# Whole branches for one and for two token tiles in the expert steps of a hybrid trunk block, with other orders for the first and last step

## The chip, the cores and the metric

The kernel runs on one core of a Trainium2 chip. The metric is the device time of one execution in microseconds (us). PE is the matrix engine, ACT, DVE and POOL are the scalar, vector and GpSimd engines, SP issues the weight loads; each runs its own queue of instructions in order and waits for the others by semaphores.

## The reference

One layer of a block on 2048 tokens of width 1024: a mixer (Mamba-2 heads beside mLSTM heads), then a mixture of experts, then a norm. Only the experts are touched here:

```python
p_group = softmax(x32 @ wg + bg); pg, g_sel = top_k(p_group, 1)
e_in = (x32 @ we + be).reshape(t, 4, 8)[:, g_sel]        # 4 groups of 8 experts
top_v, top_i = top_k(e_in, 2); gates = softmax(top_v) * pg
ids = (g_sel * 8 + top_i).reshape(-1); order = argsort(ids); xs = xf[order // 2]
hg = ragged_dot(xs, w_gate, sizes); hu = ragged_dot(xs, w_up, sizes)     # 1024 -> 512
ys = ragged_dot(silu(hg) * hu, w_down, sizes)                            # 512 -> 1024
y = segment_sum(ys * gates, tok);  out = rmsnorm(x + y, norm_f_w)
```

## The kernel before

**Tiles.** Each of the 32 experts gets the tokens that chose it in tiles of 128. All have a first tile; how many have a second is known only on the chip. `ns[i]` counts an expert's tokens in blocks of 64: over 2 there is a second tile, and at 3 only half of it is filled. A test of `ns[i]` is a branch that PE, ACT, DVE and POOL each take on their own. The trace shows which tests were taken: no second tile for experts 0 to 7, 10, 11, 13, 14, 16, 24, 27 and 29, a full one for 21 and 22, a half one for the rest.

**Weights.** Each expert has 12 pieces of 512 KB (8 of gate and up, 4 of down). SP loads a piece into one of RAW = 6 buffers (`mraw`), ACT casts it (`hi`, L652), DVE subtracts the cast (`lo`, L653): float32 products are made of three passes (hi times hi, hi times lo, lo times hi; `passes`, L763). For a half second tile two products suffice (`both`, L775). WK = 14 pairs of hi and lo are held.

**Steps.** `manual_schedule` keeps the written order on every engine. Step i runs the letters of ORDER (HEAD for i = 0, LAST for i = 31); each letter issues a piece of work on all engines concerned, and a dot feeds one weight piece (cast and subtract). In a step, A and C are the two halves of the first tile's gate and up products (24 products each), B and D those of the second tile. H turns (transposes on PE, L753, then splits the result into hi on ACT, L237, and lo on DVE, L238) the previous expert's activations h, K those of the second tile. X turns the gathered tokens `xg0` of the next expert, Y those of its second tile. a and b are the activations of the first and second tile (b of a half tile ends on POOL, L791). d and e are the two halves of the previous expert's down product, g those of its second tile; results are copied to `pv`. P adds `pv` to the token rows in memory (`accd`, L837), Q does so for the second tile. F gathers the tokens of expert i + 2 into `xg0` and, behind a test, `xg1` (L740, L880); E reads its count. r, s and m finish the rows of an earlier group of experts, 256 at a time: r gathers them (`f`), s makes their squares on ACT (L827) and the factor r on DVE and POOL (L833, L195, L201 to L204), m scales on DVE (L929) and writes.

**Skipped tests.** B, K, D, b, Y, g, Q and F hold a test each:

```python
            def whole_or_half(k, full, half):
                with tc.If(ns[k] > 2):
                    with tc.If(ns[k] < 4) as c:
                        half()
                    with c.Else():
                        full()
```

Where a test on PE is not taken, PE's sequencer runs a semaphore instruction that brings the count of PE's products up to where the skipped ones would have brought it (L1048 EVENT_SEMAPHORE in the trace).

Of the kernel before, what the change touches and what calls it, by code (L numbers as in the profile page):

```python
# [8 lines left out]
F32 = mybir.dt.float32  # L9
# [27 lines left out]
RAW, WK = 6, 14  # L37
ENGS = (mybir.EngineType.PE, mybir.EngineType.Activation, mybir.EngineType.DVE, mybir.EngineType.Pool)

ORDER = '.A.EB.HKC..r.Xa..D.b.dYePFzsg..Qm'  # L40
HEAD = 'AEBX....C.ar....D.bdYeF'
LAST = 'HKd..e..PgQ..tA..B..C...uayDhkbdKlejfvogwxq'
NQ = 4
FIRST, START = 6, 8
WB = 5
# [7 lines left out]
def hybrid_block_kernel(ctx, tc, x, norm1_w, w_in, ssd_conv_w, ssd_conv_b, ssd_dt_bias, ssd_a_log,  # L53
# [25 lines left out]
    def sc(shape, name):  # L79
        return ps_s.tile(shape, F32, name=name, tag="sc")  # L80
# [552 lines left out]
    def moe(x1, x1s, rs):  # L633
# [105 lines left out]
        def gather(dst, src, at):  # L739
            return G.indirect_dma_start(out=dst, out_offset=None, in_=src,  # L740
                                        in_offset=bass.IndirectOffsetOnAxis(ap=at, axis=0),
                                        bounds_check=S - 1, oob_is_err=False)

        def pair(n, name):
            return [mp.tile([128, n, 128], F32R, name=name + p) for p in "hl"]

        def turn(dst, src):

            hi, lo = dst
            for q in range(hi.shape[1] // 4):  # L750
                p = sc([128, 4, 128], "mt")
                for k in range(4):
                    PE.transpose(p[:, k, :], src[:, (4 * q + k) * 128:(4 * q + k) * 128 + 128], ident)  # L753
                split(hi[:, 4 * q:4 * q + 4, :], lo[:, 4 * q:4 * q + 4, :], p)

        def entry(at):
            en = mp.tile([128, 8], I32, name="en", bufs=10)
# [101 lines left out]
        def pull_down():  # L859
            return [p for u in pull(2) for p in u]  # L860
# [10 lines left out]

        def fetch(i):

            d = gather(xgs[0], x1d, eti[:, 0, seq[i]:seq[i] + 1])
            if i:
                fetch1(i)
            return d

        def fetch1(i):
            with tc.If(ns[i] > 2):  # L880
                gather(xgs[1], x1d, ens[i][1][0])

        d = fetch(0)
        for f in lows[:4]:
            f()
        xs[0] = [pair(KD, "x") for t in range(2)]
        turn(xs[0][0], xgs[0])
        for f in lows[4:]:
            f()
        feed(START - FIRST)  # L890
# [9 lines left out]
            with c.Else():  # L900
                turn(xs[0][1], xgs[1])
        fetch(1)
        sq = mp.tile([128, 2], F32, name="sq", bufs=1)
        V.memset(sq, 1.0)
        for t in pvs[1:] + fs:
            G.memset(t, 0.0)
# [47 lines left out]
            group_rows(g, q)  # L954


        gl, NW = NG - 1, 4
        sql, rl = (mp.tile([128, 2 * NQ], F32, name=n, bufs=1) for n in ("sql", "rl"))
        enl = mp.tile([128, 2 * NQ, 8], I32, name="enl", bufs=1)
        fl, gt = [], []  # L960
# [44 lines left out]
        def last_more():  # L1005
# [3 lines left out]
            with tc.If(ng > n):  # L1009
# [4 lines left out]
                for t in range(2):  # L1014
# [2 lines left out]
                    apart(d, outs)  # L1017
                    outs.append(d)

        def expert_out():  # L1020

            def second(f):
                with tc.If(ns[NE - 1] > 2):  # L1023
                    f(1)
# [7 lines left out]
            second(lambda t: square(pvs[t], sq[:, t:t + 1]))  # L1032
            norm(r, sq, False)
            out_rows(0)
            second(out_rows)

        def parts(i):

            j = i - 1
            late, cur = i > 0, i < NE  # L1040
            if i + 1 < NE:
                xs[i + 1] = [pair(KD, "x") for t in range(2)]
            w, wd = [], []
            fin = 0 <= group(i)[0] < NG - 1 and group(i)[1] < NQ
            rows = (lambda t: gt[t]) if j == NE - 1 else lambda t: None
# [8 lines that stand above are left out]
            def upper(t, q):  # L1054
                if t == 0:
                    w[:] = pull_up()
                    up(0, xs[i][0], w, q)
                else:
                    whole_or_half(i, lambda: up(1, xs[i][1], w, q), lambda: up_half(xs[i][1], w, q))

            def act1():
                whole_or_half(i, lambda: act(1, hs[i][1], ens[i][1]), lambda: act_half(hs[i][1], ens[i][1], V if i == NE - 1 else G))

            def turn_h():
                ht[j] = [pair(4, "h") for t in range(2)]
                turn(ht[j][0], hs[j][0])

            def act0():
                hs[i] = [mp.tile([128, T], F32, name="h") for t in range(2)]
# [23 lines left out]
            return dict(  # L1093
                E=(i + 2 < NE, lambda: entries(i + 2)), F=(i + 2 < NE, lambda: fetch(i + 2)),
                A=(cur, lambda: upper(0, 0)), B=(cur, lambda: upper(1, 0)), C=(cur, lambda: upper(0, KD // 2)),
                D=(cur, lambda: upper(1, KD // 2)), b=(cur, act1), a=(cur, act0), X=(i + 1 < NE, turn_x),
                Y=(i + 1 < NE, lambda: whole_or_half(i + 1, lambda: turn(xs[i + 1][1], xgs[1]),
                                                     lambda: turn_half(xs[i + 1][1], xgs[1], KD))),
                H=(late, turn_h), K=(late, lambda: whole_or_half(j, lambda: turn(ht[j][1], hs[j][1]),
                                                               lambda: turn_half(ht[j][1], hs[j][1], 4))),  # L1100
                d=(late, lambda: downer(0)), e=(late, lambda: downer(1)), g=(late, down_second),
                P=(late, lambda: puti(j, 0)), Q=(late, put1), r=(fin, lambda: group_count(i)),
                s=(fin, lambda: group_norm(*group(i))), m=(fin, lambda: group_out(*group(i))), z=(1 < i < 6, lambda: enlist(en, sl, i - 2, 2)), t=(True, last_rows), u=(True, last_rows2),
                y=(True, lambda: last_squares(0, 1)), k=(True, lambda: last_squares(2)),
                l=(True, lambda: last_squares(3, 4, 5)), j=(True, lambda: square(pvs[0], sq[:, 0:1])),
                f=(True, last_norm), v=(True, lambda: last_out((0, 1))), w=(True, lambda: last_out((2, 3))),
                x=(True, lambda: last_out((4, 5))), o=(True, last_more), q=(True, expert_out))

        held = 0
        for i in range(NE):  # L1110
            acts = parts(i)
            if i == NE - 2:
                last_entries()
            if i == NE - 1:
                end = parts(NE)
            for c in ORDER if 0 < i < NE - 1 else LAST if i else HEAD:
                if c == ".":
                    feed(min(1, WK - len(ahead) - held))
                    continue
                if c == "h":  # L1120
                    acts["H"], acts = end["H"], dict(end, D=acts["D"], b=acts["b"])
                    c = "H"
                ok, f = acts[c]
                if ok:
                    f()
                    held += {"A": 4, "C": 4, "d": 2, "e": 2, "B": -4, "D": -4, "g": -4}.get(c, 0)
# [374 lines left out]
```

## Time and profile before

| | |
|---|---|
| median of 3 runs | 2982.71 us (2981.85 to 2984.62) |
| profiled execution | 2980.81 us, span 2979.0 us |
| mean granted clock of PE | 0.982 of full speed |
| PE busy over the span | 94% |
| DVE, ACT, POOL busy | 71%, 50%, 22% |
| experts | from 2079 us to the last product at 2953 us |

A matrix product is pipelined: the trace gives 0.39 us for one of 512 columns, but in a dense row the starts lie 0.23 us apart. A bracket at the end of a timeline row is the time in which the engine had nothing to do ahead of it, with what ended that time; PEq is PE's own sequencer. The first products of the steps that are spoken of start at 2101.70 (step 1), 2392.84 (13), 2464.75 (16), 2546.62 (19), 2577.82 (20), 2791.26 (27) and 2846.42 us (29).

### The profile page before, as it was taken

To read this page: it belongs to the slowest core of one execution; us is meant where nothing else is said; L and a number is where in the kernel's file an instruction comes from. 1 tells how busy PE (TensorE), PEld (TensorE's weight loads), DVE (VectorE), ACT (ScalarE), POOL (GpSimd) and SP (SyncE) were. 2 spreads that over 40 slices of the span, in tenths; PEclk is the share of its full clock that TensorE was granted. 3 is DMA by queue.
4 is the path that set the end of the run, shared out by engine and by line. 5 is a ranking of instruction groups with operands and counts; after the bars stand their busy time and mean duration, and the time that the engine had idled before them with its cause. 6 is when DMAs were issued, how large, how long until landed. Compare 5 with 4: busy or idle time off the path is not lost. (4 is left out here: it accounts for less than half of the span.)

```text
span 2979.0 us, 41255 instructions
## 1 busy us (share of the span) xinstructions
PE 2803.4 (94%) x13444; PEld 2219.6 (75%) x13444; DVE 2130.0 (71%) x4043; ACT 1488.4 (50%) x2330; POOL 669.2 (22%) x723
## 2 busy tenths in 40 slices
PE   7999999999999999999999999998889899999995
PEld 5778877777887777788787778786667677787764
DVE  6796487688658678855867875675777777757774
ACT  5544345454434544543454454443666666655663
POOL 1431010362101035200004510001122422421433
PEclk9999999999999999999999999998999999999998
DMA  4222322422322242232224122134898998978993
GB/s 152 69 67 90 92 77 73 140 81 71 92 78 78 78 155 59 71 99 73 84 72 163 50 92 93 57 101 149 300 317 300 292 310 290 295 228 270 295 305 103
DMA packets 228916, 436.52 MB, mean 147 GB/s; under 512 B 38591, under 2 KB 38667, under 8 KB 228640
## 3 DMA queue, kind: packets, MB, share of 16 engines
q1 hardware_dynamic: 206640, 380.88, 38.8%
q0 software_dynamic: 22000, 52.22, 6.6%
q8 instruction: 142, 2.33, 0.3%
q14 instruction: 134, 1.10, 0.1%
HBM read 400.84 MB, written 54.95 MB: 153 GB/s over the span
## 5 line engine op out<-in xcount | busy, mean ns | idle before, releaser
L653 DVE TENSOR_TENSOR lo<-mraw,hi 128x1024 fp32r<-128x1024 f32 x384 | 454.9, 1231 | 80.9 <-ACT hi L652 68.0
L240 ACT ACTIVATE whi<-raw,pcol 128x512 fp32r<-128x512 f32 x416 | 295.0, 721 | 346.5 <-PE acc L278 147.0
L241 DVE SCALAR_TENSOR_TENSOR wlo<-raw,pcol,whi 128x512 fp32r<-128x512 f32 x416 | 318.7, 781 | 199.3 <-ACT whi L240 198.6
L652 ACT CAST hi<-mraw 128x1024 fp32r<-128x1024 f32 x384 | 383.6, 1052 | 79.6 <-DMA mraw<-in_exp_w_up_dram 37.0
L276 PE MATMUL acc<-hh,whi 128*128 128x512 f32 x896 | 365.3, 408 | 0.8 <-ACT whi L240 0.8
L276 PE MATMUL acc<-hh,wlo 128*128 128x512 f32 x896 | 356.8, 400 | 7.6 <-DVE wlo L241 7.6
L276 PE MATMUL acc<-hl,whi 128*128 128x512 f32 x896 | 359.8, 402 | 0.0
L278 PE MATMUL acc<-whi,hh 128*128 128x512 f32 x768 | 311.0, 405 | 2.0 <-ACT craw L289 2.0
L278 PE MATMUL acc<-whi,hl 128*128 128x512 f32 x768 | 310.2, 404 | 0.0
L278 PE MATMUL acc<-wlo,hh 128*128 128x512 f32 x768 | 308.5, 404 | 0.0
L278 PE MATMUL acc<-whi,mh 128*128 128x512 f32 x512 | 204.4, 399 | 0.0
L278 PE MATMUL acc<-whi,ml 128*128 128x512 f32 x512 | 203.4, 397 | 0.0
L278 PE MATMUL acc<-wlo,mh 128*128 128x512 f32 x512 | 203.2, 398 | 0.0
L276 PEld LDWEIGHTS acc<-hh,wlo 128*128 128x128 f32 x896 | 168.9, 189 | 45.7 <-DVE wlo L241 10.2
L290 POOL COPY hist<-craw 128x3 f32<-128x3 f32 x112 | 40.5, 362 | 717.9 <-ACT craw L289 717.6
L276 PEld LDWEIGHTS acc<-hh,whi 128*128 128x128 f32 x896 | 169.4, 189 | 34.5 <-issue 3.1
L276 PEld LDWEIGHTS acc<-hl,whi 128*128 128x128 f32 x896 | 169.6, 189 | 32.2 <-issue 2.6
L288 POOL COPY craw<-hist 128x3 f32<-128x3 f32 x112 | 70.2, 630 | 477.0 <-DVE ir L427 361.2
L278 PEld LDWEIGHTS acc<-whi,hh 128*128 128x128 f32 x768 | 146.2, 190 | 35.6 <-ACT craw L289 3.8
L278 PEld LDWEIGHTS acc<-wlo,hh 128*128 128x128 f32 x768 | 145.6, 190 | 35.2 <-DVE wlo L241 2.0
L278 PEld LDWEIGHTS acc<-whi,hl 128*128 128x128 f32 x768 | 146.2, 190 | 31.8 <-issue 1.0
L837 POOL DMA_INDIRECT accd<-pv,eti x46 | 85.6, 1860 | 356.4 <-ACT hi L652 140.3
(431 smaller groups left out, 6147.6 us busy)
## 6 DMA issues: line engine op xcount, KB each, us to landing
raw<-in_w_in_dram SPq DMA_DIRECT2D x208, 512.0 KB, 3.6
mraw<-in_exp_w_gate_dram SPq DMA_DIRECT2D x128, 512.0 KB, 6.5
mraw<-in_exp_w_up_dram SPq DMA_DIRECT2D x128, 512.0 KB, 7.1
mraw<-in_exp_w_down_dram SPq DMA_DIRECT2D x128, 512.0 KB, 5.6
raw<-in_w_out_dram SPq DMA_DIRECT2D x64, 512.0 KB, 3.6
xi<-in_x_dram SPq DMA_DIRECT2D x16, 512.0 KB, 5.9
x<-in_x_dram SPq DMA_DIRECT2D x4, 2048.0 KB, 8.7
accd<-x SPq DMA_DIRECT2D x16, 512.0 KB, 5.1
```

The source lines that it names most:

```text
L240: A.activation(hi, src, AF.Copy, scale=w)
L241: V.scalar_tensor_tensor(lo, src, w, hi.bitcast(F32), op0=OP.mult, op1=OP.subtract)
L276: mm = PE.matmul(acc[i], b[:, s], a, start=f, stop=e)
L278: mm = PE.matmul(acc[i], a[:, s], b, start=f, stop=e)
L288: G.tensor_copy(raw[:, 0:3], hist[:, ct, :])
L290: h = G.tensor_copy(hist[:, ct, :], raw[:, T:T + 3])
L652: A.copy(hi, raw)
L653: low = lambda: V.tensor_tensor(lo, raw, hi.bitcast(F32), op=OP.subtract)
L837: return G.indirect_dma_start(out=accd, out_offset=bass.IndirectOffsetOnAxis(ap=en[0], axis=0), in_=pvs[t], in_offset=None, bounds_check=S ...
```

## The change

Per step the tests on PE become two. `uppers` (c) holds the first tile's second half, and in its branch for two tiles the turn of the second tile's tokens and both halves of its products. `downers` (n) holds the previous expert's downs, and in the branch for two tiles the turn of the second h and its downs. Both branches contain the first tile's work, written twice. The second tile's gather leaves F and is issued behind c of its own step's predecessor (G). b stands behind n. HEAD turns the next tokens on PE (T) ahead of C and splits them (S) behind a, with six dots ahead of C; a Silu on two numbers is put ahead of the experts, and two of the early subtractions wait for the first gather. At the end all six tiles of the last group are multiplied by the norm's weight early (two of them on POOL), and squares and stores stand in another order.

```diff
-ORDER = '.A.EB.HKC..r.Xa..D.b.dYePFzsg..Qm'
-HEAD = 'AEBX....C.ar....D.bdYeF'
-LAST = 'HKd..e..PgQ..tA..B..C...uayDhkbdKlejfvogwxq'
+ORDER = '.A.E.H.cG.r.Xa...nbPFzs...Qm'
+HEAD = 'AEB......TCaS.r...D.bGF'
+LAST = 'HKd.Ze.PgQ..tA..B..C....uayDhkbpdKlejfgv+owxq'
...
-            d = gather(xgs[0], x1d, eti[:, 0, seq[i]:seq[i] + 1])
-            if i:
-                fetch1(i)
-            return d
+            return gather(xgs[0], x1d, eti[:, 0, seq[i]:seq[i] + 1])
...
-        for f in lows[:4]:
-            f()
+        for n, f in enumerate(lows[:4]):
+            low = f()
+            if n > 1:
+                after(low, [d])
...
+        V.memset(sq, 1.0)
+        A.activation(sq, sq, AF.Silu)
...
-        gl, NW = NG - 1, 4
+        gl, NW = NG - 1, 2 * NQ - 2
...
-                    V.tensor_tensor(fl[t], fl[t], nf, op=OP.mult)
+                    (V if t < 4 else G).tensor_tensor(fl[t], fl[t], nf, op=OP.mult)
...
+            def branch(k, two, one):
+
+                with tc.If(ns[k] > 2) as c2:
+                    with tc.If(ns[k] < 4) as c:
+                        two(True)
+                    with c.Else():
+                        two(False)
+                with c2.Else():
+                    one()
+
+            def uppers():
+
+                w2 = pull_up()
+
+                def one():
+                    up(0, xs[i][0], w2, KD // 2)
+
+                def two(half):
+                    if half:
+                        turn_half(xs[i][1], xgs[1], KD)
+                    else:
+                        turn(xs[i][1], xgs[1])
+                    one()
+                    for q, ww in ((0, w), (KD // 2, w2)):
+                        if half:
+                            up_half(xs[i][1], ww, q)
+                        else:
+                            up(1, xs[i][1], ww, q)
+                branch(i, two, one)
+
+            def downers():
+
+                wd.extend(pull_down())
+                wd.extend(pull_down())
+
+                def one():
+                    for n in range(2):
+                        down(0, ht[j][0], wd[4 * n:4 * n + 4], n)
...
+                branch(j, two, one)
...
+            ps = []
+
+            def split_x():
+                for q, p in enumerate(ps):
+                    turn_split(xs[i + 1][0], q, p)
...
+                T=(True, lambda: ps.extend(turned(xgs[0], q) for q in range(2))), S=(True, split_x),
...
+                c=(cur, uppers), n=(late, downers), G=(i + 1 < NE, lambda: fetch1(i + 1)),
...
-                l=(True, lambda: last_squares(3, 4, 5)), j=(True, lambda: square(pvs[0], sq[:, 0:1])),
+                p=(True, lambda: last_squares(3)), l=(True, lambda: last_squares(4, 5)),
+                j=(True, lambda: square(pvs[0], sq[:, 0:1])),
```

PE in a step of the middle, before: the end of D's branch (products into `pg_18328` and `pu_18329`, the second tile), all of b's test, and the first down product into `pyd_18330`.

```order
L763 MATMUL pu_18329<-hi,xl 128x512
L763 MATMUL pu_18329<-lo,xh 128x512
L1049 UNCONDITIONAL_BRANCH
L1048 UNCONDITIONAL_BRANCH
L1048 COMPARE_AND_BRANCH
L1049 COMPARE_AND_BRANCH
L1049 UNCONDITIONAL_BRANCH x2
L1048 UNCONDITIONAL_BRANCH
L763 MATMUL pyd_18330<-hi,hh 128x512
```

The same place of the changed kernel: the last products of c's branch for one tile, the test of G, the turn of the next tokens, and the head of n with its branch for a half tile.

```order
L768 MATMUL pu_18327<-hi,xl 128x512
L768 MATMUL pu_18327<-lo,xh 128x512
L1068 UNCONDITIONAL_BRANCH
L882 COMPARE_AND_BRANCH
L882 UNCONDITIONAL_BRANCH x2
L750 MATMUL mt<-ident,xg_18063 128x128 x8
L1068 COMPARE_AND_BRANCH
L1069 COMPARE_AND_BRANCH
L802 MATMUL mt<-ident,h 128x64 x4
L768 MATMUL pyd_18330<-hi,hh 128x512
```

Between the turn of the tokens and the downs one test is left, and its two outcomes both hold the downs.

ACT in a step that finishes rows of a group, before: the squares of `f` (s), then the second tile's copies of `pv` (g). The second tile's activation (b) is issued 16 rows ahead of the first of these.

```order
L923 COMPARE_AND_BRANCH
L827 ACTIVATE o,sq<-f_18324 128x1024
L827 ACTIVATE o,sq<-f_18325 128x1024
L923 UNCONDITIONAL_BRANCH x2
L1048 COMPARE_AND_BRANCH
L1049 COMPARE_AND_BRANCH
L804 COPY pv_18323<-pyd_18330 64x512
L804 COPY pv_18323<-pyd_18331 64x512
```

After: the copies of n's branch end, then b (L791 to L795 for a half tile, L815 for a full one), then the squares.

```order
L826 COPY pv_18322<-pyd_18330 128x512
L1068 UNCONDITIONAL_BRANCH
L1053 COMPARE_AND_BRANCH
L1054 COMPARE_AND_BRANCH
L791 COPY h<-pg_18328 64x512
L792 ACTIVATE u<-pu_18329,etf 64x512
L795 ACTIVATE h<-h,etf 64x512
L1054 UNCONDITIONAL_BRANCH
L815 ACTIVATE h<-pg_18328,etf 128x512
L1054 UNCONDITIONAL_BRANCH
L1053 UNCONDITIONAL_BRANCH
L929 COMPARE_AND_BRANCH
```

Here b and the squares have moved behind all copies of the step's down products.

ACT in the first step, before: the split of the next tokens (`xh`), five casts, the table of the Silu, and the activation a.

```order
L1049 UNCONDITIONAL_BRANCH x2
L1048 UNCONDITIONAL_BRANCH
L237 CAST xh<-mt 128x512 x2
L652 CAST hi<-mraw 128x1024 x5
L810 ACT_TABLE_LOAD
L810 ACTIVATE h<-pg_18326,etf 128x512
L652 CAST hi<-mraw 128x1024 x4
```

After:

```order
L1054 UNCONDITIONAL_BRANCH x2
L1053 UNCONDITIONAL_BRANCH
L652 CAST hi<-mraw 128x1024 x6
L815 ACTIVATE h<-pg_18326,etf 128x512
L237 CAST xh<-mt 128x512 x2
L652 CAST hi<-mraw 128x1024 x4
```

Six casts stand ahead of the activation and of the split instead of none ahead of the split and five between, and the table load is gone from here.

## Rows read from the trace of the kernel before

**Rows 1.** Windows of step 0, steps 2 to 7, steps 8 to 30.

```profile
core 0: us, PE busy (x) PEld busy (x) DVE busy (x) ACT busy (x) POOL busy (x), PEclk, DMA share, GB/s
2079.30:2101.70 22.40, 14.21 (x57) 11.14 (x57) 12.19 (x14) 9.50 (x12) 4.18 (x5) 0.80 0.64 202
2124.97:2255.40 130.43, 116.01 (x513) 87.50 (x513) 103.19 (x102) 88.66 (x104) 30.85 (x17) 1.00 0.96 323
2255.40:2910.00 654.60, 624.10 (x2875) 479.98 (x2876) 475.43 (x511) 404.20 (x521) 197.81 (x201) 0.99 0.88 285
```

**Rows 2.** PE's sequencer on L1048, 2100 to 2910 us: ns min/median/max, first, last.

```profile
L1048 PEldq EVENT_SEMAPHORE  x76: 51/51/51, 2110.1 to 2904.6; - x76
```

**Rows 3.** Timeline of PE in step 13: start, duration, line, out<-in, idle before.

```profile
2398.19 0.39 PE L763 MATMUL pu<-lo,xh 128*128 128x512 f32 x1
2398.88 0.63 PE L753 MATMUL mt<-ident,h 128*128 128x128 f32 x4 [0.30 <-PEq L1048]
...
2405.41 1.03 PE L753 MATMUL mt<-ident,xg 128*128 128x128 f32 x8
2406.90 0.50 PE L763 MATMUL pyd<-hi,hh 128*128 128x512 f32 x1 [0.46 <-ACT xh L237]
...
2409.55 0.40 PE L763 MATMUL pyd<-lo,hh 128*128 128x512 f32 x1
2410.10 0.47 PE L763 MATMUL pyd<-hi,hh 128*128 128x512 f32 x1
```

**Rows 4.** Timeline of ACT in step 0.

```profile
2093.85 1.07 ACT L237 CAST xh<-mt 128x512 fp32r<-128x512 f32 x2 [12.87 <-PE pu L763]
2094.81 4.84 ACT L652 CAST hi<-mraw 128x1024 fp32r<-128x1024 f32 x5
2099.66 1.28 ACT L810 ACT_TABLE_LOAD   x1
2100.96 0.69 ACT L810 ACTIVATE h<-pg,etf 128x512 f32<-128x512 f32 x1
```

**Rows 5.** Timeline of PE, first product of step 1.

```profile
2101.70 0.80 PE L763 MATMUL pg<-hi,xh 128*128 128x512 f32 x1 [7.89 <-ACT h L810]
```

**Rows 6.** Timeline of POOL, end of step 18.

```profile
2540.18 1.28 POOL L791 TENSOR_TENSOR h<-u,h 64x512 f32<-64x512 f32 x1 [13.77 <-ACT h L790]
2544.64 1.62 POOL L837 DMA_INDIRECT accd<-pv,eti  x1 [3.17 <-DVE v L833]
2546.56 1.03 POOL L740 DMA_INDIRECT xg<-x1d,eti  x1 [0.31 <-DVE pv L807]
...
2548.92 0.74 POOL L201 TENSOR_TENSOR rs_t<-rs_i 128x2 f32<-128x2 f32 x1
```

**Rows 7.** Timeline of ACT, the last copy of step 18.

```profile
2546.82 0.58 ACT L804 COPY pv<-pyd 64x512 f32<-64x512 f32 x1 [1.15 <-PE pyd L775]
```

**Rows 8.** Timeline of ACT, the act of a half tile in step 19.

```profile
2569.52 0.58 ACT L786 COPY h<-pg 64x512 f32<-64x512 f32 x1
...
2571.38 0.72 ACT L790 ACTIVATE h<-h,etf 64x512 f32<-64x512 f32 x1 [0.69 <-DVE h L788]
```

**Rows 9.** Timeline of DVE, start of step 19.

```profile
2553.61 2.48 DVE L929 SCALAR_TENSOR_TENSOR f<-f,r,nf 128x1024 f32<-128x1024 f32 x2 [2.86 <-POOL r L204]
2556.01 3.49 DVE L653 TENSOR_TENSOR lo<-mraw,hi 128x1024 fp32r<-128x1024 f32 x3
```

**Rows 10.** Timeline of PE in step 11; of DVE and PE in step 29.

```profile
2350.18 1.09 PE L753 MATMUL mt<-ident,xg 128*128 128x128 f32 x8 [1.38 <-DVEq L1048]
...
2857.78 2.48 DVE L929 SCALAR_TENSOR_TENSOR f<-f,r,nf 128x1024 f32<-128x1024 f32 x2 [4.39 <-POOL r L204]
...
2864.32 1.97 PE L753 MATMUL mt<-ident,xg 128*128 128x128 f32 x8 [5.18 <-DVE hl L238]
```

**Rows 11.** Line L740, 2100 to 2910 us: issue to landing of the gathers.

```profile
DMA to landing us min/median/max: 4.6/7.8/9.9
```

**Rows 12.** Sequencer of PE on line L1130, a branch to the kernel's far end.

```profile
L1130 PEldq COMPARE_BRANCH  x1: 3785/3785/3785, 2951.4 to 2951.4; - x1
```

More of the change, by code (lines that the diff above doesn't have):

```diff
@@ L745, in pair, with turned, turn_split @@
             return [mp.tile([128, n, 128], F32R, name=name + p) for p in "hl"]
-        def turn(dst, src):
[L749 to L754, printed above, removed]
+        def turned(src, q):
+            p = sc([128, 4, 128], "mt")
+            for k in range(4):
+                PE.transpose(p[:, k, :], src[:, (4 * q + k) * 128:(4 * q + k) * 128 + 128], ident)
+            return p
+        def turn_split(dst, q, p):
+            split(dst[0][:, 4 * q:4 * q + 4, :], dst[1][:, 4 * q:4 * q + 4, :], p)
+        def turn(dst, src):
+            for q in range(dst[0].shape[1] // 4):
+                turn_split(dst, q, turned(src, q))
         def entry(at):
@@ L883, in moe @@
         d = fetch(0)
-        for f in lows[:4]:
-            f()
+        for n, f in enumerate(lows[:4]):
+            low = f()
+            if n > 1:
+                after(low, [d])
         xs[0] = [pair(KD, "x") for t in range(2)]
         turn(xs[0][0], xgs[0])
+        sq = mp.tile([128, 2], F32, name="sq", bufs=1)
+        V.memset(sq, 1.0)
+        A.activation(sq, sq, AF.Silu)
         for f in lows[4:]:
@@ L902, in moe @@
         fetch(1)
-        sq = mp.tile([128, 2], F32, name="sq", bufs=1)
         V.memset(sq, 1.0)
@@ L1018, in last_more, with second @@
                     outs.append(d)
+        def second(f):
+            with tc.If(ns[NE - 1] > 2):
+                f(1)
         def expert_out():
-            def second(f):
-                with tc.If(ns[NE - 1] > 2):
-                    f(1)
             def out_rows(t):
@@ L1030, in out_rows @@
                 outs.append(d)
-            second(lambda t: square(pvs[t], sq[:, t:t + 1]))
             norm(r, sq, False)
@@ L1059, in upper, with two @@
                     whole_or_half(i, lambda: up(1, xs[i][1], w, q), lambda: up_half(xs[i][1], w, q))
+            def branch(k, two, one):
[28 more added lines that the diff above has]
+                        down(0, ht[j][0], wd[4 * n:4 * n + 4], n)
+                def two(half):
+                    if half:
+                        turn_half(ht[j][1], hs[j][1], 4)
+                    else:
+                        turn(ht[j][1], hs[j][1])
+                    one()
+                    for n in range(2):
+                        if half:
+                            down_half(ht[j][1], wd[4 * n:4 * n + 4], n)
+                        else:
+                            down(1, ht[j][1], wd[4 * n:4 * n + 4], n)
+                branch(j, two, one)
             def act1():
+                hs[i].append(mp.tile([128, T], F32, name="h"))
                 whole_or_half(i, lambda: act(1, hs[i][1], ens[i][1]), lambda: act_half(hs[i][1], ens[i][1], V if i == NE - 1 else G))
@@ L1068, in act0 @@
             def act0():
-                hs[i] = [mp.tile([128, T], F32, name="h") for t in range(2)]
+                hs[i] = [mp.tile([128, T], F32, name="h")]
                 act(0, hs[i][0], ens[i][0])
@@ L1096, in parts @@
                 D=(cur, lambda: upper(1, KD // 2)), b=(cur, act1), a=(cur, act0), X=(i + 1 < NE, turn_x),
-                Y=(i + 1 < NE, lambda: whole_or_half(i + 1, lambda: turn(xs[i + 1][1], xgs[1]),
-                                                     lambda: turn_half(xs[i + 1][1], xgs[1], KD))),
+                T=(True, lambda: ps.extend(turned(xgs[0], q) for q in range(2))), S=(True, split_x),
+                Z=(cur, lambda: whole_or_half(i, lambda: turn(xs[i][1], xgs[1]),
+                                              lambda: turn_half(xs[i][1], xgs[1], KD))),
+                c=(cur, uppers), n=(late, downers), G=(i + 1 < NE, lambda: fetch1(i + 1)),
                 H=(late, turn_h), K=(late, lambda: whole_or_half(j, lambda: turn(ht[j][1], hs[j][1]),
@@ L1122, in moe @@
                     c = "H"
+                if c == "+":
+                    second(lambda t: square(pvs[t], sq[:, t:t + 1]))
+                    continue
                 ok, f = acts[c]
@@ L1125, in moe @@
                     f()
-                    held += {"A": 4, "C": 4, "d": 2, "e": 2, "B": -4, "D": -4, "g": -4}.get(c, 0)
+                    held += {"A": 4, "c": -4, "C": 4, "d": 2, "e": 2, "B": -4, "D": -4, "g": -4}.get(c, 0)
         order.close()
```

## The prediction

> **What bounds the kernel now.** I read the windows first. In steps 8 to 30 PE is busy 624.1 of 654.6 us while DVE has 475 and ACT 404; the DMA engines are busy 0.88 of the time [rows 1]. PE is the bound there, and what can be won is its idle time, 30 us and the slow restarts. In steps 2 to 7, which have one tile each, PE has 116.0 of 130.4 us, but the DMA engines are at 0.96 and move 323 GB/s [rows 1]: there the weights come in at the pace of the step, and PE's waits are partly the room that the stream needs. Step 0 is neither: PE 14.2 of 22.4 us, DMA 0.64, and the clock at 0.80 [rows 1].
>
> Then I asked PE's sequencer what a test costs that is not taken. 76 of them end in a semaphore instruction of 51 ns [rows 2]. Its own length is nothing; what counts is that it stands behind products that must have ended. The timeline of step 13 shows it: the turn of h starts 0.69 us after the last product of A instead of 0.23, so 0.46 late; the first down product comes 1.49 us after the start of eight transposes that take 0.88 in a dense row, 0.6 late; the second half of the downs comes 0.55 after its predecessor, 0.32 late [rows 3]. The same reading at all 76 places (start to start, less the dense pitch) adds up to 37.2 us: 15.8 at 33 places in steps 1 to 7, 21.4 at 43 places in steps 8 to 30.
>
> Next the stalls that are there already. In steps behind one that finishes rows of a group (m), the turn of the next tokens X waits for DVE: five such waits, 1.38 us the first, 5.18 the last, 14.0 together [rows 10].
>
> **The change part by part.**
>
> Tests on PE. The new branches write the first tile's work into both outcomes, and the skipped count travels on a product of the branch. A test not taken then has no instruction that waits for the drain, so in steps 8 to 30 the 21.4 us go, and with them a slower second product behind some of the drains (0.31 in place of 0.23 us), about 1. Steps 8 to 30: **+22**, between 18 and 25.
>
> Steps 1 to 7 lose 15.8 us of drains too, but the stream is 4% short of full there [rows 1], and 4% of some 154 us is 6. Faster casts in step 0 give the stream a start (next paragraph), so I take **+7**, between 0 and 10.
>
> First step. ACT sat idle for 12.87 us, until the last product of C released the buffer of the next tokens; then the split, five casts (4.84 us), a table load (1.28 us) and a came one behind the other [rows 4], and PE waited 7.89 us for a [rows 5]. In the new order six casts fall into the idle time, the table is loaded earlier, and a (0.7 us) needs only the end of C; the split of the next tokens adds 1.07 us [rows 4] to the wait of the second product alone. PE's wait falls to some 1.5 us: **+6.5**, between 0 (if the raw pieces aren't there in time; the share of 0.64 speaks against it) and 8.
>
> The second tile's activation b is the part that I think costs. It used to run beside the downs; now its place on ACT is behind the copies of the downs, which end as the next step begins. All times now from the first product of the next step. The last copy ended at 0.78 (2547.40 less 2546.62) [rows 7]; b of a half tile takes 2.58 us to the end of its Silu [rows 8], so 3.4; POOL's product 1.28 [rows 6], 4.7; then, in POOL's queue behind it, P 1.62 and the gather F, each with 0.3 of issue between [rows 6]: F starts at 6.6. It started at -0.06 in step 18 [rows 6].
>
> (a) F gathers the next step's own tokens. X of a one-tile step comes 11.4 us in (two halves of 24 products at 0.23, and a turn). A gather lands 4.6 to 9.9 us from issue, 7.8 in the middle [rows 11]: at 14.4, so 3 us late, in the steps behind a half tile that have one tile and no m before them: 10, 13, 16, 24. With landings from 4.6 up some come in time: **-6**, between 0 and -15.
>
> (b) In a step that finishes rows, POOL's chain for r stands behind F: from 2548.92 to the start of m at 2553.61 it took 4.7 us [rows 6, 9]. F ends at 7.6, so m starts at 12.4 and ends at 14.9, where it ended at 9.5 (2556.09) in step 19 [rows 9]. DVE does m in its order, ahead of three subtractions (3.49 us for three [rows 9]) and the split of h; X came 4.06 us after the end of m in step 29 [rows 10]. So X of a one-tile step is possible at 19.0 instead of 11.4. In a two-tile step the turn of the second tile now stands ahead of C and its low part is wanted at 11.9, and it has the same queue ahead of it. Both wait some 7.5. Four steps follow a half tile with rows to finish (19, 20, 27, 29): 30 us. Behind a one-tile step with rows there is no b; m ends near 10.5 as now and X, which no drain delays any more, waits 3; step 12 keeps its 4. Together 37, less the 14.0 of today [rows 10]: **-23**, between 0 (if POOL or ACT run b early enough) and -30.
>
> A full second tile is turned in two quarters ahead of C, where PE can do nothing else. The second quarter wants the buffer that the split of h frees, and DVE comes to that behind four or five subtractions (1.16 each [rows 9]), some 2.5 us after PE is there: two steps, **-5**, between 0 and -7.
>
> Two tests on PE in place of five leave the sequencer less to do; the last step and the tail move work among ACT, POOL and DVE: squares and products of 1 to 2 us earlier, the second tile's turn (Z) later. I find no wait that they end for sure, and price them at **0**, between -4 and +4: the tail is a chain from the last product through `pv`, the square, the norm and the store, and that chain keeps its links.
>
> The sum: 22 + 7 + 6.5 - 6 - 23 - 5 = +1.5 us. The profiled execution took 2980.81, 1.9 below the median of the runs shown: 2979.3 on its scale, 2981.2 on the median's. I take **2979.5**.
>
> A rule that speaks against the change: the new one-tile branch lies behind two whole branches for two tiles, some 130 products for c, so a jump goes far. The trace has one far jump on PE, of 3.785 us [rows 12], against 0.45 at most for the tests of the steps. PE's sequencer runs 1.7 us ahead of PE, so 2 us would be left per far jump not hidden; with 16 one-tile steps 32 us. [...]
>
> **The rivals.**
>
> One: the late b hides. If b's pieces go ahead while PE still works on the second tile's downs, or the chain on POOL is shorter than in step 18, (a), (b) and the full tile cost little, a third of the sum above (11 of 34). For it speaks that PE has several us of second-tile downs behind the first tile's, and that a stall in one step lets the casts run ahead for the next. Against it: the order on ACT is fixed. It gives 2980 - 35 + 11, so about 2957, and with all hidden 2946.
>
> Two, on the other side: the late m decides. From an m that ends later than 7 us into the next step on, each further us is a us of PE. At the ends of the bounds (a -15, b -30, full tile -7) against gains of 31 (22, 3, 6), it gives 2982 + 21 = 3003.
>
> Three: the far jump is not hidden, about 3011, or in part 2995. Against it speaks that the tests of before jump as well, over products of a half and a full tile, without more than 0.45 us.
>
> Four: the change doesn't do what it says: a drain is needed somewhere else on PE (a branch's end, or the first product that carries the count). Then the 22 and 7 shrink to a third while the costs stay: near 2999. Against it: the branches that are taken today have no such gap.
>
> **How the numbers follow.** A change of 0.2%, 6 us, is about what a measurement of this kernel tells from none. The sum, with its own range of 2969 to 2991: 0.40, of that 0.12 faster, 0.22 the same, 0.06 slower. Rival one: 0.30, all but 0.02 of it faster. Rival two: 0.18, 0.15 slower, 0.03 the same. Rival three 0.06, four 0.06, 0.10 slower and 0.02 the same. That makes 0.40 faster, 0.29 the same, 0.31 slower. The range from 2955 to 3004 leaves out the best of rival one and the worst of three.
>
> **What the changed profile would show.** The semaphore instruction on PE behind a test not taken is gone, and the down products follow the transposes at the dense pitch. Step 1 starts near 2095. In steps 2 to 7 the DMA share goes up to 0.97 or more and not all of the drains' time returns. In steps 19, 20, 27 and 29 PE stands 5 us or more for DVE, with m ending 14 to 15 us in; if it ends by 10, the -23 is wrong. In steps 10, 13, 16 and 24 X waits for the gather. A branch of 2 to 4 us on PE's sequencer would bear out rival three. What would make the forecast wrong above all is (b): it is the largest cost, worked out from one step's chain.

## The result, and the profile after

The changed kernel takes 3088.91 us (median of 4, 3088.29 to 3093.57) against 2983.66 for the one before on the same chip: ratio 1.0351, 95% interval 1.0338 to 1.0365. It is 105 us slower, where 2979.5 with a range up to 3004 was forecast. First the page: span, and busy time of PE; PE does the same 13444 products in a longer span.

```profile
span 3087.4 us, 40519 instructions
PE 2825.7 (92%) x13444; PEld 2253.2 (73%) x13444; DVE 2129.4 (69%) x4042; ACT 1490.3 (48%) x2333; POOL 688.1 (22%) x725
```

The windows of step 0, steps 2 to 7 and steps 8 to 30 (columns as in [rows 1]) say where:

```profile
2082.82:2097.94 15.12, 14.09 (x56) 10.85 (x57) 13.34 (x15) 11.16 (x14) 5.32 (x5) 0.88 0.93 335
2117.80:2247.25 129.45, 112.62 (x505) 91.41 (x504) 100.13 (x101) 85.33 (x100) 30.33 (x17) 0.96 0.96 323
2247.25:3018.00 770.75, 647.15 (x2871) 504.82 (x2870) 476.36 (x513) 407.40 (x525) 221.16 (x201) 0.91 0.76 243
```

Step 0 is 7.3 us shorter than in [rows 1]. Steps 2 to 7 take 129.5 us in place of 130.4. Steps 8 to 30 take 116 us more (to the same point of step 31), at a granted clock of 0.91 in place of 0.99 and with the DMA engines less busy. Step 1 is 3.4 us shorter (19.9 for 23.3). From the start of the last product to the end of the span it is 26.8 us, 26.5 before.

The drains are gone: on the new tests PE's sequencer has branches only, none of the semaphore instructions of [rows 2]. But the longest of its branches now takes 4.5 us (below: duration in ns, smallest, middle and largest).

```profile
L1068 PEldq COMPARE_BRANCH  x60: 65/216/4516, 2101.1 to 3001.8; - x60
```

What came in their place stands in PE's timeline, some of the waits of steps 10, 11, 12, 19, 21 and 27, and one at the head of step 31:

```profile
2325.11 1.94 PE L750 MATMUL mt<-ident,xg 128*128 128x128 f32 x8 [5.74 <-DMA xg<-x1d,eti]
2330.56 0.66 PE L802 MATMUL mt<-ident,h 64*128 64x64 f32 x4 [3.50 <-DVE xl L238]
...
2360.82 0.45 PE L750 MATMUL mt<-ident,xg 128*128 128x128 f32 x1 [6.68 <-DVEq L1068]
...
2390.69 0.79 PE L780 MATMUL pg<-hi,xh 128*128 128x512 f32 x1 [8.40 <-DVE xh L238]
2391.28 0.63 PE L780 MATMUL pg<-lo,xh 128*64 128x512 f32 x1
2391.70 0.63 PE L780 MATMUL pu<-hi,xh 128*128 128x512 f32 x1
...
2600.61 0.80 PE L780 MATMUL pg<-hi,xh 128*128 128x512 f32 x1 [8.35 <-DVE xh L238]
...
2675.87 1.08 PE L750 MATMUL mt<-ident,xg 128*128 128x128 f32 x4 [5.63 <-DVE hl L238]
...
2897.26 1.09 PE L750 MATMUL mt<-ident,xg 128*128 128x128 f32 x4 [8.66 <-DVEq L1068]
...
3013.84 0.46 PE L802 MATMUL mt<-ident,h 64*128 64x64 f32 x4 [3.14 <-POOL h L796]
```

The waits over steps 8 to 30 are read start to start, less the dense pitch:

- Seven waits behind m (steps 11, 12, 19, 20, 27, 28 and 29) are 55.7 us. Before, they were 14.8 by the count of the prediction. But only four of its five waits, 12.4 us, are X's behind m; the fifth, 2.5 us in step 27, is the wait of the second tile's downs for ACT's copy of `pv`, and it is gone now (its row of before stands below).
- X waits 22.4 us for the gather in steps 10, 13, 14, 16 and 24 (almost none before).
- n's turn of the second h waits for the split of X in 14 steps, 29.0 us.
- The full tile's turn in c waits twice, 10.3 us.
- Behind the long ones of these waits PE's starts lie further apart for some us. Behind the 8.40 us the next seven starts lie 0.39 to 0.59 us apart, five of them 0.43, in place of 0.23, at a granted clock of 0.51 (2390.69 to 2393.80); in the 3.20 us behind that it is 1.00. Over the 3.1 us behind each of the other five waits of 5.63 to 8.66 us shown above it is 0.50. Starts that are 0.05 to 0.28 us late add up to 41.0 us, 19.8 before. Most of these 21 us are starts 0.42 to 0.43 us apart: 113 of them, 18 before.

```profile
2815.37 0.50 PE L775 MATMUL pyd<-hi,hh 128*128 128x512 f32 x1 [2.33 <-ACT pv L821]
```

The chain that the prediction worked out is there to 0.2 us. ACT, POOL and DVE at the end of step 18 (the next step starts at 2579.90):

```profile
2580.10 0.58 ACT L809 COPY pv<-pyd 64x512 f32<-64x512 f32 x1 [1.23 <-PE pyd L780]
...
2582.03 0.72 ACT L795 ACTIVATE h<-h,etf 64x512 f32<-64x512 f32 x1 [0.28 <-DVE h L793]
```

```profile
2582.89 1.29 POOL L796 TENSOR_TENSOR h<-u,h 64x512 f32<-64x512 f32 x1 [14.47 <-ACT h L795]
2584.35 1.62 POOL L842 DMA_INDIRECT accd<-pv,eti  x1 [0.17 <-issue]
2586.28 1.86 POOL L740 DMA_INDIRECT xg<-x1d,eti  x1 [0.30 <-PE mt L802]
...
2592.11 0.20 POOL L204 TENSOR_TENSOR r<-rs_t,r 128x2 f32<-128x2 f32 x1
```

```profile
2592.34 2.48 DVE L935 SCALAR_TENSOR_TENSOR f<-f,r,nf 128x1024 f32<-128x1024 f32 x2 [2.85 <-POOL r L204]
2594.74 3.49 DVE L653 TENSOR_TENSOR lo<-mraw,hi 128x1024 fp32r<-128x1024 f32 x3
...
2599.88 0.68 DVE L238 TENSOR_TENSOR xh<-mt,xh 128x512 fp32r<-128x512 f32 x1
```

F starts 6.4 us in (6.6 worked out), m at 12.4 and ends at 14.9. The last row, a low part that c's products want, releases PE at 2600.61. In step 11, which starts at 2342.60 with no b ahead of it, m ends 12.9 us in:

```profile
2353.04 2.48 DVE L935 SCALAR_TENSOR_TENSOR f<-f,r,nf 128x1024 f32<-128x1024 f32 x2 [2.57 <-POOL r L204]
```

### The profile page after: what moved, and what is told of

Read it like the earlier page. It is cut to its first block, busy times and chain, and to the rows that moved or that the text cites. A ratio compares the mean times of both kernels' runs of the same rounds, so it can differ in the third digit from the quotient of the medians.

```text
span 3087.4 us, 40519 instructions
## 1 busy us (share of the span) xinstructions
PE 2825.7 (92%) x13444; PEld 2253.2 (73%) x13444; DVE 2129.4 (69%) x4042; ACT 1490.3 (48%) x2333; POOL 688.1 (22%) x725
## 3 DMA queue, kind: packets, MB, share of 16 engines
q14 instruction: 128, 1.05, 0.1%
## 5 line engine op out<-in xcount | busy, mean ns | idle before, releaser
L842 POOL DMA_INDIRECT accd<-pv,eti x46 | 97.1, 2111 | 332.8 <-ACT hi L652 187.5
```

Source lines behind the costliest of these rows:

```text
L842: return G.indirect_dma_start(out=accd, out_offset=bass.IndirectOffsetOnAxis(ap=en[0], axis=0), in_=pvs[t], in_offset=None, bounds_check=S ...
```

## The experiments

Each is told by its edit, of which only the lines that matter are shown; orders are the letters of a step. Runs 1 to 3, 5, 6 and 15 start from the changed kernel, the others from the one before. Ratios are to runs of the kernel before on the same chip; where two runs are compared with each other, their medians can come from two chips, whose medians of the kernel before lie up to 7 us apart.

**1. b ahead of the downs** (with a buffer more for the second tile's h).

```diff
-ORDER = '.A.E.H.cG.r.Xa...nbPFzs...Qm'
+ORDER = '.A.E.H.cG.r.Xab...nPFzs...Qm'
```

> The changed kernel with b put ahead of n (order Xab...nPFzs in place of Xa...nbPFzs), and a buffer of its own more for the second tile's h, so that b needn't wait for n's turn. Theory of the late b: POOL's product is done before the downs end, P, F, the chain for r and m all come some 4 to 5 us earlier in steps behind a half tile; m ends near 10 us into the next step in place of 14.9, the seven waits of PE behind m shrink from 54.6 us to 15 to 25, the waits of X for the gather in steps 10, 13, 16 and 24 from 18 to under 6, and the slower clock behind these waits goes with them: 3020 to 3040 us. Rival, the branches themselves (far jumps, more code): under 10 us of change, 3080 to 3090.

3080.49 us (ratio 1.0321, 1.0303 to 1.0338): 8 us, not 50. POOL's product is 12 us earlier against the next step's start (2578.83), but P isn't:

```profile
2569.91 1.29 POOL L796 TENSOR_TENSOR h<-u,h 64x512 f32<-64x512 f32 x1 [4.51 <-ACT h L795]
2581.14 1.62 POOL L842 DMA_INDIRECT accd<-pv,eti  x1 [9.94 <-ACT o L832]
```

P adds the first tile's `pv`, whose copy on DVE ended at 2575.48. It starts after the second tile's last copy, at 2580.32. So it does in steps 2 to 30 of this run: where P is not held in POOL's own queue, it starts 0.8 us behind the last copy that n's branch makes, whatever the bracket names. m now ends 12.9 us in, in six of the seven steps. So in steps 19 and 27 the late b is two of the five us by which m moved.

**2. F behind a.**

```diff
+ORDER = '.A.E.H.cG.r.XaF...nbPzs...Qm'
```

> The changed kernel with F put behind a (order XaF...nbPzs), so the gather of the next tokens goes out as soon as their buffer is read. Theory that POOL's queue order makes the gather late: no wait of X for the gather is left (37 us in steps 1 to 24), and the chain for r is 2 us shorter in seven steps: 3040 to 3060 us; steps 1 to 7 gain only some 6 of their 16 us, since the stream of weights is near full there. Rival, landings are slow because the DMA engines are full: the wait stays in steps 1 to 7 and 3075 or more in all.

3067.95 us (1.0284, 1.0267 to 1.0301): 21 us less, short of the theory's 30 to 50. No wait of X names the gather any more, but in steps 10, 13, 16 and 24 PE only comes sooner to the next wait, n's turn: the waits of the half turns for the split of X grow from 26.6 to 36.0 us.

**3. The turn K apart from n.**

```diff
+ORDER = '.A.E.HK.cG.r.Xa...nbPFzs...Qm'
```

> The changed kernel with the turn of the second tile's h taken out of n and done behind H in a test of its own (K), as before. Theory that PE stands in n because the turn of h finds both buffers of the transposes taken by X: the waits of 1.06 to 5.3 us between X and n in the steps behind a second tile (some 27 us) go, the two steps behind full tiles too, 16 skipped tests come back at 0.31 us each: 3055 to 3070 us. Rival, the wait is only moved, since the downs want the same split: 3085 or more.

3130.04 us (1.0482, 1.0465 to 1.05): 41 us slower: on the rival's side (3085 or more), but the wait moved to another place than it said. The half turn in c now stands behind two turns, H and K, and waits 86.8 us in twelve steps. Six long branches, three of them 4.7 to 6.7 us, stop PE for 24 us too.

**4. The first step alone**, in the kernel before: the new HEAD with T and S, and the early Silu.

```diff
-HEAD = 'AEBX....C.ar....D.bdYeF'
+HEAD = 'AEB......TCaS.r...D.bdYeF'
```

> The kernel before with the first step of the change alone (the next tokens turned ahead of C and split behind a, six dots ahead of C, the table of the Silu loaded early). By the trace of the change, step 1 starts 15.1 us after step 0 in place of 22.4: theory that this gain lasts, 2976 us (faster by 5 to 7). Rival, the stream of weights takes it back in steps 1 to 7: 2981 to 2984.

2977.1 us (0.9975, 0.9966 to 0.9985): the gain of the first step lasts, some 8 us. Runs 7 to 14, 16 and 17 are made on this kernel, so they are read against 2977.

**5 and 6. The second tile's tokens turned in the step before** (Y), with their gather (V, a letter of its own here) behind F, in the changed kernel; **then F behind a as well.**

```diff
+ORDER = '.A.E.H.c.r.Xa...nYbPFVzs...Qm'
...
+ORDER = '.A.E.H.c.r.XaF...nYbPVzs...Qm'
```

> The changed kernel with the turn of the second tile's tokens taken out of c and put back into the step before, in a test of its own behind n (nYbPF), its gather behind F as in the kernel before. Theory that c makes PE wait because the split of the second tile's tokens stands in DVE's queue behind m and the feeds and is wanted at once: the waits of PE inside c (35.7 us in 8 steps, 10.3 in the two full ones) go, with the slower clock behind them, some 5 us of skipped tests come back: 3030 to 3050 us. Rival, DVE is just as late for the next turn: the wait moves to X or n and the time stays above 3070.

> As the run before, and F behind a as well. Theory that the late gather and the late turn are two costs of their own: another 15 to 25 us less, 3010 to 3030. Rival, they are one wait that only changes its name: within 8 us of the run before.

3056.06 (1.0245, 1.0227 to 1.0262) and 3033.19 us (1.0166, 1.0149 to 1.0183). The late turn, with its late gather, costs 33 us, and the late F 23 beside it: two costs of their own.

**7 and 8. One branch alone**, in the kernel before with the new first step: c (7), n with its turn (8).

```diff
-ORDER = '.A.EB.HKC..r.Xa..D.b.dYePFzsg..Qm'
+ORDER = '.A.E.HKc..r.Xa...b.dYePFzsg..Qm'
...
+ORDER = '.A.EB.HC..r.Xa..D.b..nYPFzs.Qm'
```

> The kernel before with the new first step, and with B, C and D alone made one branch (first tile's second half, then both halves of the second tile; the turns K and Y and the downs stay as they were). Theory that the branch form is good in itself, and that only what was moved with it costs: the drains behind A and between X and d go (some 1.0 us in 16 one-tile steps, half of it in steps 1 to 7 eaten by the stream): 2964 to 2971 us. Rival, the long branch costs more than the drains, by its jumps and because b comes later: 2977 to 2990.

> The kernel before with the new first step, and with K, d, e and g alone made one branch (a buffer more for the second tile's h, b ahead of it as before). Theory that the downs' branch is what costs: P waits for the end of the whole branch, m comes 3 to 5 us later in the steps that finish rows, and the turn of the second h finds both transpose buffers taken by X: 2995 to 3015 us. Rival, n is harmless with b in its old place: 2960 to 2972.

3020.43 (1.0124, 1.0107 to 1.0141) and 3046.6 us (1.0213, 1.0191 to 1.0234), so 43 and 70 us slower than run 4, and beyond every figure expected. In run 7 two things show. First, a long branch of PE's sequencer, with PE in step 3 (its duration in ns, then the timeline):

```profile
L1070 PEldq COMPARE_BRANCH  x1: 6646/6646/6646, 2146.9 to 2146.9; - x1
```

```profile
2145.93 0.60 PE L750 MATMUL mt<-ident,h 128*128 128x128 f32 x4
2153.63 0.80 PE L768 MATMUL pg<-hi,xh 128*128 128x512 f32 x1 [7.10 <-issue]
```

Five branches over 1 us, all in steps with one tile, where the code for two is jumped over, cost PE 17 us. While the one shown runs, the DMA view of 2146.9 to 2153.6 has one packet, of 16 KB, in the queue that the profile calls instruction:

```profile
q8 instruction: 1, 0.02, 0.8%
```

It starts at 2151.18 and takes 0.88 us; the branch ends 1.5 us behind it. PE also stops for 4.38 us in step 6, up to 2228.14, with no long branch in the trace but such a packet that landed 1.4 us earlier. Second, the second tile's downs wait for the copy of the first tile's on ACT, 2.3 us in step 18, with b between X and that copy and no product of D to give ACT time:

```profile
2562.87 0.39 PE L768 MATMUL pyd<-lo,hh 128*128 128x512 f32 x1
2565.57 0.79 PE L780 MATMUL pyd<-hi,hh 128*128 128x512 f32 x1 [2.31 <-ACT pv L826]
```

**9 and 10. The same orders as short tests**, without any branch that holds the first tile's work.

```diff
+ORDER = '.A.E.HKCBD..r.Xa...b.dYePFzsg..Qm'
...
+ORDER = '.A.EB.HC..r.Xa..D.b..KdegYPFzs.Qm'
```

> The kernel before with the new first step, and with the second tile's products in the order of c (B and D one behind the other after C, b further back), but as two short tests of their own, no branch that holds the first tile's work. Theory that the order costs (the second tile's products no longer stand between X and the downs, so ACT and DVE are behind when the downs end): 2995 to 3010 us, some 17 us of long jumps less than c's whole branch at 3020. Rival, the whole branch itself costs everything (jumps, and consumers that wait for its end): 2975 to 2983.

> The kernel before with the new first step, and with K, d, e and g in the order of n, as short tests of their own (a buffer more for the second tile's h). Theory of the order: the turn of the second h waits for X's split and the downs end late for P in steps behind a two-tile step: 3010 to 3030 us against 3047 for the whole branch, since the long jumps (15 us) and P's wait for the end of the branch go. Rival, the whole branch itself: 2975 to 2990.

3048.26 (1.0205, 1.0188 to 1.0222) and 3023.23 us (1.0133, 1.0116 to 1.015). No branch in the steps is long. The order alone costs 71 and 46 us against run 4; the theory of run 9 had at most 33, that of run 10 holds. With it, c's whole branch is 28 us better than two short tests, n's is 23 worse than its tests.

**11. F behind a in the kernel before with the new first step** (its second gather, V, stays behind P).

```diff
+ORDER = '.A.EB.HKC..r.XaF..D.b.dYePVzsg..Qm'
```

> The kernel before with the new first step, and F alone moved behind a (its second tile's gather stays behind P). Theory that POOL's queue is what makes X wait for the gather and m come late in the kernel before too: the five waits of X for the gather (5 us) go and m comes 1.4 us earlier in seven steps: 2963 to 2972 us. Rival, the waits of the kernel before are set by the stream of weights: 2975 to 2979, no gain.

2966.27 us (0.9932, 0.9915 to 0.9948), the fastest of all: 0.7% under the kernel before. Its windows of steps 2 to 7 and 8 to 30:

```profile
2118.95:2243.27 124.32, 115.11 (x512) 87.90 (x512) 103.81 (x102) 88.88 (x103) 26.81 (x17) 1.00 0.99 341
2243.27:2898.80 655.53, 626.90 (x2880) 482.60 (x2881) 475.63 (x511) 403.65 (x520) 196.38 (x200) 0.99 0.89 284
```

Steps 2 to 7 take 124.3 us against 130.9 in run 4 and 130.4 in [rows 1], with the stream at 0.99, and X no longer waits for its gather there. The share of 0.96 was not the stream's limit but held back by the gather.

**12. c without its branch for a full tile**, on run 7. Experts 21 and 22 get a half tile's products only.

```diff
-                    with tc.If(ns[k] < 4) as c:
-                        two(True)
-                    with c.Else():
-                        two(False)
+                    two(True)
```

> The run e7_c_only without the branch for a full second tile in c: experts 21 and 22 then get the products of a half tile only, so half of their second tile isn't computed, which takes some 7 us of PE work away. The jump of the one-tile path over the two-tile code becomes half as long. Theory that the 5 long branches of e7 (17 us of PE's time) come from the length of the jump: none is left over 1 us, 2994 to 3000 us. Rival, that any branch of this kind is long now and then: 3010 to 3015, the 7 us of left out work alone.

3008.28 us (1.007, 1.0054 to 1.0087). Short of the theory's time, but no branch in the steps is over 0.43 us:

```profile
L1070 PEldq COMPARE_BRANCH  x45: 65/174/423, 2105.4 to 2919.7; - x45
```

That points to the length of the code that is jumped over, though the inner test is gone with it. Of the 12 us, 7.0 are the work left out in steps 21 and 22; the jumps, 17 us as PE's idle time, gave back about 5 in the end, since PE then waits for the next gather: 22.8 us in steps 2 to 30, 6.4 in run 7.

**13. s ahead of P**, on run 11.

```diff
+ORDER = '.A.EB.HKC..r.XaF..D.b.dYesPVzg..Qm'
```

> The run e11_f_split with s put ahead of P, so that POOL's chain for r starts as soon as the squares are there and P and the second gather come behind it. Theory that the place of that chain in POOL's queue sets when m ends: m ends 3 to 4 us earlier in the steps behind one that finishes rows (5 to 6 us in, from 8.6 to 9.6), and the 11 us for which X still waits behind m fall under 5: 2957 to 2962 us. Rival, m waits for the rows' gather or for DVE's own queue, and the later P holds up the next copies: 2965 to 2972.

2983.7 us (0.999, 0.9981 to 0.9999): 17 us worse than run 11, beyond the rival too. m ends 6.5 us in behind single steps as the theory said, but where steps that finish rows follow each other s waits for their gather: in step 29 m ends 17.8 us in, 13.0 in run 11, and P comes behind it all, at 2857.34, 16 us in. X waits 9.11 us for DVE, behind m:

```profile
2863.04 1.75 PE L750 MATMUL mt<-ident,xg 128*128 128x128 f32 x7 [9.11 <-DVE hl L238]
```

**14. c's branch with b behind P and F behind a**, on run 7.

```diff
+ORDER = '.A.E.HKc..r.XaF...d.YePbVzsg..Qm'
```

> The run e7_c_only with F behind a and with b behind P. Theory that most of the 43 us of e7 are the order on ACT (three casts and b stand between X and the copy of the first downs, now that no products of D give it time: 27 us of waits for pv): with b behind the copies 2985 to 2997 us, and what is left are the long jumps. Rival, the whole branch itself costs: 3010 or more.

2977.42 us (0.9968, 0.9955 to 0.9981): 43 us less than run 7, below the theory's range, and 11 over run 11. One dot moved behind d with them. Long branches in steps 3 and 6 stop PE for 5.8 us.

**15. The change mended in four places.**

```diff
+ORDER = '.A.E.H.c.r.XabF...nYsPVz...Qm'
```

> The changed kernel with four orders mended at once: the turn of the second tile's tokens back in the step before, F behind a, b ahead of n (with the buffer that it needs), s ahead of P. Both whole branches, the first and the last step stay. Theory that the places of these letters are what costs, and the branches little: 2995 to 3012 us. Rival, what is lost is in the branches (P waits for the end of n, the second tile's products no longer stand between X and the downs): 3020 to 3035.

3038.27 us (1.0183, 1.0167 to 1.0198): the rival's side, no better than run 6. PE's idle time between X and n's turn is 40 us, 26 in the changed kernel.

**16 and 17. n beside the mended c**, without and with the turn of the second h.

```diff
+ORDER = '.A.E.HKc..r.XaF....nYPbVzs..Qm'
...
+ORDER = '.A.E.Hc..r.XaF....nYPbVzs..Qm'
```

> The run e14_c_b_late with d, e and g made one branch n as well, but the turn of the second h left in K, ahead of c. Both whole branches are there, the turns and the places of b and F are the old or mended ones. Theory that n costs by its turn, which stands right behind X with both transpose buffers taken: without it 2975 to 2992 us. Rival, n costs because P and the copies wait for the end of the whole branch: 3005 or more.

> The same with the turn of the second h inside n, as in the change (K gone). Theory of the turn: PE waits 1.2 us or more between X and n in each step behind a two-tile step, 40 us in all with the slower clock: 3015 to 3035 us. Rival: within 8 us of the run without the turn.

3011.06 (1.0073, 1.0056 to 1.009) and 3007.57 us (1.0064, 1.0047 to 1.008). My theory of the turn falls: n costs 30 to 34 us over run 14 whether it holds the turn or not. With it PE waits between X and n, 25.7 us for the half turns (in a traced execution of 3019.83 us, 12 over run 17's median). Without it PE waits 17.3 us for ACT's copies of `pv`. DVE and then POOL at the end of step 18 of run 16, which ended at 2553.11:

```profile
2549.31 0.68 DVE L828 COPY pv<-pyd 128x512 f32<-128x512 f32 x1
...
2552.80 0.68 DVE L812 TENSOR_TENSOR pv<-pyd,pv 64x512 f32<-64x512 f32 x1 [1.19 <-ACT pv L809]
```

```profile
2554.30 1.62 POOL L842 DMA_INDIRECT accd<-pv,eti  x1 [10.55 <-DVE xh L238]
```

P needs the first row and starts behind the second. In run 14, with d, e and g apart, it starts 1.2 us before the next step, at 2538.49 for 2539.68; here 1.2 us after.

Apart from the first and last step, run 17 has the order of run 6 with b behind P and two dots moved, one from ahead of c to behind it, one from behind s to ahead of n. It is 26 us faster, and its waits between X and n in steps 10, 13, 16 and 24 are 9 us, 29 in run 6. Which of the moves does it was not tried.

## Why the prediction was wrong

Right were the drains (the 22 us of steps 8 to 30 came back, and nothing of them stayed), the first step (6.5 forecast, 7.3 in the trace, some 8 by run 4), the tail at 0, and the mechanism of (b): m ends 14.9 us in, as worked out. Rival four is out.

Where it failed, by its steps:

- **(b), -23, was mis-sized**: 40.9 us more of waits (55.7 less 14.8). The prediction read 14.0 us of idle time before as X's waits behind m; only 11.7 of it were. The four steps listed cost 33.7 us, near the 30 worked out. But steps 11 and 12 were priced at 7 and step 28 at nothing, on the ground that no b stands there; they cost 22.0. The step missed that P, and F and the chain for r behind it, wait for the end of n's branch: in step 11, with no b ahead of it but a second tile in n, m ended 12.9 us in, not 10.5, and X waited 6.7 us; step 28 is alike (13.0). In step 12 m was no later than before (15.0 us in, 15.9 before); there the second tile's turn, which now stands ahead of C, came to wait for it.
- **(a), -6, and steps 1 to 7, +7**: the gather is late in the four steps listed (19.1 us), in step 14 and in all of steps 2 to 7, which were not. X waited for it 22.4 us in steps 8 to 30 and 17.0 in steps 2 to 7, where what the drains gave back went there: 129.5 us in place of 130.4. Steps 1 to 7 gained 4.4 us, 3.4 of them in step 1, and the DMA share did not rise above 0.96. I read the DMA share of 0.96 there as the stream's limit; run 11 shows 0.99 and 124.3 us once F is moved.
- **The full tile, -5**: 10.3 us.
- **Not in the sum at all**: the turn in n, right behind X, whose split it waits for (29.0 us). The working followed both turns into the branches but asked only of c's what DVE had ahead of it. Runs 16 and 17 show that this wait is where the time is lost, not what the turn costs: without the turn n is no cheaper.
- **Not in the sum**: PE's slower starts behind the waits, 21 us, with a granted clock of 0.50 to 0.51 behind the six of 5.63 to 8.66 us shown above. Every wait was priced at its own length.
- **Rival three** was half right. Ten branches of 1.8 to 4.5 us are there, on PE alone, but cost PE only 4 us in the changed kernel. Where PE does not wait for them, its sequencer is far enough ahead: in step 10 a branch of 3.4 us starts at 2310.16, and the first product behind it starts at 2313.69 without a wait. In run 7 the semaphore of K's skipped test stands just ahead of c (2146.57) and takes that lead away: 7.10 us of wait for a branch of 6.65. The lead of 1.7 us that the prediction took off each jump is neither. No one figure holds for it: in step 13 of the kernel before, D's test starts 1.72 us ahead of the first down product (2405.18 for 2406.90), the test of r (L916) 4.07 us ahead of X (2401.34 for 2405.41). In runs 3, 7 and 8 the branches cost 15 to 24 us.

  In all 19 profiles the branches of over 1 us on PE's sequencer from the experts on, 138 of them, end 1.3 to 1.7 us behind the landing of a 16 KB packet in queue q8; of those under 0.46 us 3% do. In the changed kernel there are eleven (the ten and one of 3.7 us on L1200), and they end 1.36 to 1.53 us behind it; the one of the kernel before [rows 12] ends 1.36 us behind it. That they wait for this packet is my reading of these distances. The length of the jump alone does not decide: beside whole branches short tests of the second tile took up to 3.4 us too (runs 5, 6, 8 and 14 to 17). Why only some of the same branches are long, no run shows.

The new costs of steps 8 to 30, 40.9 + 22.4 + 10.3 + 29.0 + 21.2, with 3.5 us of other waits in c (steps 8, 9, 18 and 26), 2.4 at long branches and 3.3 for the late b's product on POOL at the head of step 31, less 21.4 of drains, make 112 of the 116 us.

The range failed with it: rival two, the worst of these mechanisms, was bounded at 3003 from the same incomplete list of waits.

What stays open: run 9 shows that c's order costs 71 us, and run 14 that with b and F moved almost none of c's cost is left, but b, F and a dot were moved together there; in a kernel without the branch F alone is worth 11. How n's 30 us split between P's wait, ACT's copies and the dots that moved with it wasn't tried; nor was the changed kernel with b behind P and nothing else moved.

## What to carry to other kernels

When tests are merged into whole branches, list what reads a result of the branch: here the scatter P waited for the branch's last copy, and all that stood behind P in POOL's queue with it. Work that was spread between products gave other engines time; put together it must be paid where they fall behind, so follow each engine's queue from the last product of the block, for every turn and copy in it. A gather whose buffer is free early belongs there in the queue, not behind a store that waits for the step's end: that one letter was worth 0.4% (run 11 against run 4) and made the fastest version of all.

## What the runs showed of the hardware that I had not expected

PE's sequencer took up to 6.7 us for some conditional branches over the code of a half and a full tile, 0.43 at most over that of a half tile alone (runs 7 and 12), while ACT, DVE and POOL had none over 0.6 us in any run. Each of the 138 branches of over 1 us ended 1.3 to 1.7 us behind the landing of a 16 KB packet of queue q8, so a narrow window of the DMA view helps to tell such a branch from a wait for another engine. And a wait of 8.4 us cost PE some 1.5 us more than its length: the seven starts behind it take 3.11 us in place of 1.61, at a granted clock of 0.51.
